# A two-block transformer kernel: the second mixer and the expert choice in two halves of the tokens, and two token tiles instead of one by gathered expert rows

## The chip, the cores and the metric

The kernel runs on one core of a Trainium2 chip. Its time is the device time of one execution in microseconds (us). A core has five engines with a queue of instructions each: TensorE (PE in the profile; PEld is its weight load), VectorE (DVE), ScalarE (ACT), GpSimd (POOL) and SyncE (SP), which here only issues transfers. Sixteen DMA engines move data between device memory (HBM) and on-chip memory. TensorE writes its products to eight accumulator banks (PSUM), each 128 partitions by 512 fp32 numbers.

## The reference

512 tokens of 1024 numbers pass two blocks, all in fp32. Block one is feed-forward, an attention mixer, feed-forward. Block two is a mixer (latent attention with 8 heads beside a retention with a state carried over chunks of 128 tokens) and then PEER, a layer of 16384 experts, each a row `u` and a row `v` of 1024 numbers:

```python
q = (xt @ w_query).reshape(T, 8, 2, 128)
s = einsum('thpd,pkd->thpk', q, sub_keys)          # 2 x 128 keys
s_top, i_top = top_k(s, 16)                        # level 1
cand = s_top[:, :, 0, :, None] + s_top[:, :, 1, None, :]
best, pos = top_k(cand.reshape(T, 8, 256), 16)     # level 2: the expert choice
eidx = ...                                         # i_top0 * 128 + i_top1, at pos
g = softmax(best)
a = gelu(einsum('thkd,td->thk', expert_u[eidx], xt))
out = einsum('thk,thkd->td', g * a, expert_v[eidx])
```

So each token uses 8 x 16 = 128 of the 16384 experts. The output is the normalised sum of the block's input and this.

## The kernel before, in words

The 512 tokens are four tiles of 128 (tiles 0 to 3). Every fp32 weight product is three products of high and low parts (`mm3`, L126 to L128): a weight tile is brought in by SyncE (`raw`, L113), and split by ScalarE into a high part (`whi`, L120) and by VectorE into the rest (`wlo`, L121).

Block one ends at about 1270 us. The second mixer (`mixer2`) runs over all four tiles: projections, attention by pairs of tile and head, retention, and the output product (`project`), with each tile normalised and transposed behind it (`boundary`). Queries and level 1 (`peer_queries`, `peer_level1`) make, for each tile, head and key half, scores on TensorE and the 16 best with VectorE (L1344 to L1348). Level 2 (`peer_level2`) is VectorE work, tile by tile.

The experts are done in two ways:

- Tiles 1 to 3 are dense: all 16384 experts for all 384 tokens, in 128 chunks of 128 experts. `emit_a(c)` splits one chunk of `u` rows (`in_euT`) and makes its products with 384 columns: 8 x 3 matmuls. The main loop over chunks multiplies the result by a gate table (`gt`, read from `dg` in device memory, L1543), splits the product and the chunk of `v` rows (`in_evp`) and adds to six accumulator halves (`acc`): 3 tiles x 2 halves x 3 matmuls of 512 columns. `peer_spread` builds the gate table of a tile out of one-hot rows on VectorE (L1375 to L1378) and 128-wide fp16 products.
- Tile 0 is gathered: GpSimd fetches, for each of the 128 places of the choice, one row for each token (`erow`, L1446, 128 rows of 4 KB, 512 KB in all). A `u` row is multiplied with the normalised tokens and summed by one VectorE instruction (L1450, here called a dot), a `v` row is added with its weight by another (L1458).

The first 78 chunks of `emit_a` run while VectorE does level 2 and the spread; all but 12 of them go to device memory (`da`) and come back in the main loop, where `emit_a` is 12 chunks ahead of `acc`. The pace of gathers is written out: `gathers(rate, after)` issues rows when enough are owed. A scheduler then sets the order in each queue, from the order of the code, its priorities and the free buffers.

Of the kernel before, what the change touches and what calls it, by code (L numbers as in the profile page):

```python
# [20 lines left out]
P = 128  # L21
S = 512
# [6 lines left out]
NF = 22  # L29
NEG = -1.0e30  # L30
# [51 lines left out]
class Body:  # L82
# [33 lines left out]
    def split(self, r, room=None):  # L116
# [4 lines left out]
        self.last_low = self.nc.vector.tensor_tensor(lo, r, hi.bitcast(F32), op=OP.subtract)  # L121
        return hi, lo
# [35 lines left out]
    def xrstd(self, t):  # L158

        return self.rstd(self.sumsq(self.xe[:, t, :D + 1], D), eps=0.0)  # L160

    def diag(self, r):

        d = self.misc.tile([P, P], F32, name="dg", tag="dg")
        self.nc.scalar.activation(d, self.idf, AF.Copy, scale=r)
        return d

    def ndiag(self, c, n):
        return self.diag(self.rstd(self.sumsq(c, n)))


    def setup(self):
# [12 lines left out]
        c = self.const  # L185
        self.front = ExitStack()
# [3 lines left out]
        self.xe = f.tile([P, NT, D + 4], F32, name="x")  # L190
        self.x = self.xe[:, :, :D]
        self.nc.vector.memset(self.xe[:, :, D:], (EPS * D) ** 0.5)
# [152 lines left out]
    def begin(self, hi, lo):  # L345
# [4 lines left out]
        with ExitStack() as st:  # L350
# [11 lines left out]
            def turned(q):  # L362
                qs = slice(2 * q, 2 * q + 2)
                self.acol(0, 1, "g_pre_ffn1", qs)
                for t in range(NT):
                    self.transposed(self.x[:, t, q * 256:(q + 1) * 256], 2, t, hi, lo, self.ac[:, 0, qs],
                                    self.mc[:, 0, qs], 2 * q, diag=dg[t])
# [11 lines left out]
            for t in range(NT):  # L379
                nc.sync.dma_start(self.x[:, t, :], a["x"][t * P:(t + 1) * P, :])  # L380
# [22 lines left out]
    def h_tiles(self):  # L403
        hi = self.hbuf.tile([P, KD, S], F32R, name="h_hi", tag="h_hi")
        lo = self.hbuf.tile([P, KD, S], F32R, name="h_lo", tag="h_lo")
        return hi, lo

# [32 lines left out]
    def boundary(self, join, scale, bias, last):  # L440


        d, h = {}, []

        def turn(t):
            if t == 0:
                h.extend(self.h_tiles())
            self.transposed(self.x[:, t, :], KD, t, *h, self.ac[:, scale], self.mc[:, bias], diag=d.pop(t))

        for t in range(NT):  # L450
            last(t)
            join(t)
            d[t] = self.diag(self.xrstd(t))
            if t in (1, 2):
                turn(t - 1)
        return h, [lambda: turn(2), lambda: turn(3)]

    def postnorm(self, t, y, grow):
# [6 lines left out]
        for hf in range(2):  # L465
# [3 lines left out]
            nc.vector.tensor_tensor(self.x[:, t, sl], self.x[:, t, sl], v, op=OP.add)  # L469


    def ffn(self, gu, dn, h, between, join, scale, bias, ps0=None):
# [3 lines left out]
        with ExitStack() as st:  # L476
# [12 lines left out]
            for f in range(NF):  # L489
# [5 lines left out]
                for n, cut in enumerate(cuts):  # L495
                    for j in range(2):
# [3 lines left out]
                        if not f and not n:  # L500
                            late_h[j]()
# [26 lines left out]
            for f in range(NF):  # L528
# [7 lines left out]
                if f < NF - 6:  # L536
                    for t in range(NT):
# [3 lines left out]
                                 lambda t: product(t, ws, by_half if t < NT - 1 else by_chunk))  # L541
# [1162 lines left out]
```

## Time and profile before

| | us |
|---|---|
| median of 3 runs (2862.94, 2867.7, 2869.01) | 2867.7 |
| the profiled execution | 2865.86 |
| its span in the profile | 2864.1 |
| TensorE busy | 2805.2 |
| VectorE busy | 2052.6 |
| ScalarE busy | 1158.3 |
| GpSimd busy | 366.7 |

The span is the stretch from the first to the last recorded instruction. "Busy" is the sum of an engine's recorded instructions; overlapping matmuls count once. DMA share is the mean busy share of the sixteen DMA engines, GB/s what they moved.

The program after 1270 us has three stages that are used below: the second mixer with its output product and the normalisations at its edges (to 1605 us), queries, both levels of choice and the spread beside the first 78 `emit_a` (to 2104 us, where the first `acc` product starts), and the main loop with the end (to 2864.1 us).

### The profile page before, as it was taken

The numbers are of one execution on the slowest core, as the hardware profiler recorded it, in microseconds if no ns is written. First come the engines' busy times: TensorE is split into PE (matmuls) and PEld (weight loads), VectorE is DVE, ScalarE is ACT, GpSimd is POOL, SyncE is SP. The second block draws the span as 40 slices with busy tenths as digits, with TensorE's granted clock in tenths as the row PEclk, the third lists the DMA queues.
The fourth block names the chain that finished last, engine by engine and source line by source line (L and its number), as shares of the span: only waits on it lengthen the run. The fifth ranks groups of instructions, "written<-read, shape, count | busy, mean of one in ns | idle before, by whom it ended". The sixth has DMA issues, their size and how long they took to land. (4 is left out here: it accounts for less than half of the span.)

```text
span 2864.1 us, 41177 instructions
## 1 busy us (share of the span) xinstructions
PE 2805.2 (98%) x15725; PEld 2414.2 (84%) x15725; DVE 2052.6 (72%) x4416; ACT 1158.3 (40%) x1946; POOL 366.7 (13%) x367
## 2 busy tenths in 40 slices
PE   8999999999999999999999999999999999999998
PEld 6877788869788877888898989899988888898996
DVE  6795246785655787225665699999967778787887
ACT  4343145333534444225522433655633333333333
POOL 0000000000000000001001001111121115433441
PEclk9999999999999999999997999999999999999999
DMA  7663221212033564321121226888899999888885
GB/s 277 226 226 138 103 74 60 92 60 89 16 138 121 194 235 177 110 103 41 67 79 47 104 78 225 295 282 314 318 334 342 324 311 358 317 314 317 298 328 193
DMA packets 152533, 553.09 MB, mean 193 GB/s; under 512 B 12368, under 2 KB 61840, under 8 KB 112400
## 3 DMA queue, kind: packets, MB, share of 16 engines
q1 hardware_dynamic: 111040, 404.25, 38.8%
q0 software_dynamic: 38848, 140.56, 13.8%
q10 hardware_dynamic: 2448, 5.65, 0.5%
q8 instruction: 123, 2.02, 0.3%
q14 instruction: 74, 0.61, 0.1%
HBM read 505.95 MB, written 44.47 MB: 192 GB/s over the span
## 5 line engine op out<-in xcount | busy, mean ns | idle before, releaser
L120 ACT ACTIVATE whi<-raw 128x1024 fp32r<-128x1024 f32 (+2 forms) x491 | 510.1, 1040 | 806.0 <-PE ps L127 385.8
L121 DVE TENSOR_TENSOR wlo<-raw,whi 128x1024 fp32r<-128x1024 f32 (+2 forms) x491 | 588.7, 1199 | 299.2 <-ACT whi L120 295.6
L126 PE MATMUL ps<-h_hi,whi 128*128 128x384 f32 (+2 forms) x1904 | 691.1, 364 | 4.7 <-ACT ga L1431 3.1
L127 PE MATMUL ps<-h_lo,whi 128*128 128x384 f32 (+2 forms) x1904 | 684.2, 359 | 0.8 <-DVE h_lo L132 0.8
L128 PE MATMUL ps<-h_hi,wlo 128*128 128x384 f32 (+2 forms) x1904 | 683.0, 359 | 0.7 <-DVE wlo L121 0.7
L126 PEld LDWEIGHTS ps<-h_hi,whi 128*128 128x128 f32 x1904 | 359.2, 189 | 37.7 <-ACT ga L1431 3.8
L128 PEld LDWEIGHTS ps<-h_hi,wlo 128*128 128x128 f32 x1904 | 359.1, 189 | 32.4 <-DVE wlo L121 1.3
L127 PEld LDWEIGHTS ps<-h_lo,whi 128*128 128x128 f32 x1904 | 359.8, 189 | 31.3 <-DVE h_lo L132 1.0
L126 PE MATMUL acc<-whi,wh 128*128 128x512 f32 x768 | 304.0, 396 | 1.7 <-ACT wh L131 1.7
L128 PE MATMUL acc<-whi,wl 128*128 128x512 f32 x768 | 304.0, 396 | 0.3 <-DVE wl L132 0.3
L127 PE MATMUL acc<-wlo,wh 128*128 128x512 f32 x768 | 303.8, 396 | 0.1
L1446 POOL DMA_INDIRECT erow<-in_eu,ids x128 | 141.8, 1108 | 648.8 <-DVE junk L1450 478.3
L131 ACT ACTIVATE wh<-wv 128x384 fp32r<-128x384 f32 x128 | 67.2, 525 | 341.1 <-issue 174.4
L1446 POOL DMA_INDIRECT erow<-in_ev,ids x128 | 166.2, 1299 | 225.2 <-DVE eacc L1458 198.5
L126 PE MATMUL ps<-whi,h_hi 128*128 128x256 f32 (+1 forms) x608 | 186.0, 306 | 0.0
L127 PE MATMUL ps<-wlo,h_hi 128*128 128x256 f32 (+1 forms) x608 | 184.0, 303 | 0.0
L128 PE MATMUL ps<-whi,h_lo 128*128 128x256 f32 (+1 forms) x608 | 183.7, 302 | 0.0
L128 PEld LDWEIGHTS acc<-whi,wl 128*128 128x128 f32 x768 | 144.5, 188 | 35.9 <-DVE wl L132 0.8
L126 PEld LDWEIGHTS acc<-whi,wh 128*128 128x128 f32 x768 | 144.3, 188 | 35.1 <-ACT wh L131 2.0
L127 PEld LDWEIGHTS acc<-wlo,wh 128*128 128x128 f32 x768 | 144.5, 188 | 33.3 <-DVE wlo L121 0.5
L1458 DVE SCALAR_TENSOR_TENSOR eacc<-erow,wgt,eacc 128x1024 f32<-128x1024 f32 x127 | 162.8, 1282 | 6.3 <-DMA erow<-in_ev,ids 3.2
L290 DVE SCALAR_TENSOR_TENSOR rows<-mraw,sil,rows 128x256 f32<-128x256 f32 x336 | 159.8, 481 | 6.5
(453 smaller groups left out, 4636.3 us busy)
## 6 DMA issues: line engine op xcount, KB each, us to landing
raw<-in_euT SPq DMA_DIRECT2D x64, 1024.0 KB
raw<-in_evp SPq DMA_DIRECT2D x64, 1024.0 KB
raw<-in_gu SPq DMA_DIRECT2D x44, 1024.0 KB
mraw<-in_wmod SPq DMA_DIRECT2D x24, 1024.0 KB
mraw<-in_wada SPq DMA_DIRECT2D x24, 1024.0 KB
dg<-gb SPq DMA_DIRECT2D x24, 1024.0 KB
gt<-dg SPq DMA_DIRECT2D x16, 1536.0 KB
raw<-in_dn SPq DMA_DIRECT2D x22, 1024.0 KB
```

What stands on the lines that cost most here:

```text
L120: self.nc.scalar.activation(hi, r, AF.Copy)
L121: self.last_low = self.nc.vector.tensor_tensor(lo, r, hi.bitcast(F32), op=OP.subtract)
L126: mm(out, l[0], r[0], start=start, stop=False)
L127: mm(out, l[0], r[1], start=False, stop=False)
L128: self.last_mm = mm(out, l[1], r[0], start=False, stop=stop)
L131: self.nc.scalar.activation(hi, v, AF.Copy)
L290: nc.vector.scalar_tensor_tensor(rows, rv[:, k, :], c, rows, op0=OP.mult, op1=OP.add)
L1446: nc.gpsimd.indirect_dma_start(out=row, out_offset=None, in_=src, in_offset=bass.IndirectOffsetOnAxis(ap=ids[:, m:m + 1], axis=0))
L1458: nc.vector.scalar_tensor_tensor(eacc, row, wg[:, m:m + 1], eacc, op0=OP.mult, op1=OP.add)
```

## The change

Block one stays. The rest is done for two halves of the tokens, `self.tt` = tiles (0, 1), then (2, 3). For tiles 0 and 1: mixer, output product (`project_half`), queries, level 1 and level 2 (`chosen`). Then the same for tiles 2 and 3, with `hook` asking for gathers of `u` rows after each split (2.0 rows) and each attention step (0.8 x 2.0). The mixer's and the query weights are brought in and split once for each half, and the keys, values and states of the first half are kept for the second. Tiles 0 and 1 are both gathered: 256 `u` rows with a dot each, and 256 `v` rows. The `v` rows are summed on TensorE, four rows in a step: eight products 32 columns wide and 512 long, one for each row and half, into four column groups of the array and two accumulator banks (`ga`), with weights spread on diagonals (`zw`). They begin when all `u` rows are done. The dense part is left with tiles 2 and 3: 256 columns in `emit_a`, four `acc` halves, 16 instead of 24 parts of the gate table. At the edges of the mixers a tile is scaled first (half on ScalarE, half on VectorE) and then transposed, where before one product with a diagonal matrix did both.

```diff
-                self.mm3(p[:, :384], (w[0][:, ks], w[1][:, ks]), (h[0][:, k, P:], h[1][:, k, P:]), k == 0, k == KD - 1)
+                self.mm3(p[:, :W], (w[0][:, ks], w[1][:, ks]), (h[0][:, k, :], h[1][:, k, :]), k == 0, k == KD - 1)
...
+        RU, RD, RW = 1.2, 2.0, 0.7
...
+        rows = gp.tile([P, 4, D], F32, name="rows")
+        self.slots += [rows[:, j] for j in range(4)]
...
+    def gather_u(self, n):
+        t, m = divmod(n, P)
+        row = self.slots[n % len(self.slots)]
+        nc.gpsimd.indirect_dma_start(out=row, out_offset=None, in_=self.a["eu"],
+                                     in_offset=bass.IndirectOffsetOnAxis(ap=self.ids[t][:, m:m + 1], axis=0))
+        junk = self.misc.tile([P, D], BF, name="junk", tag="sg")
+        nc.vector.scalar_tensor_tensor(junk, row, 1.0, self.x(t), op0=OP.mult, op1=OP.mult,
+                                       accum_out=self.act[t][:, m:m + 1])
...
+        def fetch(k):
+            t, j = divmod(k, 32)
+            held[k] = [self.slots[(4 * k + g) % 8] for g in range(4)]
+            for g in range(4):
+                nc.gpsimd.indirect_dma_start(out=held[k][g], out_offset=None, in_=a["ev"],
+                                             in_offset=bass.IndirectOffsetOnAxis(ap=self.idt[t][:, 32 * g + j:32 * g + j + 1], axis=0))
+        def weigh(k):
...
+            for hf in range(2):
+                for g in range(4):
+                    nc.tensor.matmul(y[t][hf][32 * g:32 * g + 32, :], z[:, j % 8, g, :], held[k][g][:, hf * 512:hf * 512 + 512],
+                                     start=j == 0, stop=j == 31)
...
+        def values(rate, after):
+            if self.got < 2 * P:
+                return
+            owed += rate
+            while done < min(owed, 64):
+                with tc.issue_after(after.ins):
+                    fetch(done)
+                if done:
+                    with tc.issue_after(self.last_mm.ins):
+                        weigh(done - 1)
+                done += 1
...
             if c < P - 3 or c == P - 1:
-                for t in range(3):
+                for t in range(2):
...
-            gathers(R2 if c < EARLY - LEAD else R3 if c < P - LEAD else R4 if c < P - TAIL else 2 * P, pace)
+            if self.got < 2 * P:
+                self.gathers(RD, pace)
+            else:
+                values(RW if c < P - FIN - 2 else 99, pace)
...
+                self.tt = (0, 1)
+                h = self.second(0, hs[0], late, old)
+                sp, v, ix = self.select(0, *h, s1)
+                self.tt = (2, 3)
+                z = self.hbuf.tile([P, 4, D], F32, name="slots", tag="h_hi")
+                self.slots = [z[:, j] for j in range(4)]
...
+                with self.later(600):
+                    for t in range(2):
+                        self.chosen(sp, t, self.peer_level2(sp, v[t], ix[t]), "ps")
+                self.hook = lambda n, after: self.gathers(n * R0, after)
+                h = self.second(1, hs[1], [], old)
```

The order of VectorE at the expert choice of the first tile, before (`cand`, `best`, `bp` are the choice, `wlo` the split of a weight tile, here of `emit_a`):

```order
L1348 MAX_INDEX pix_14951<-pv_14948,t_15966 128x8
L121 TENSOR_TENSOR wlo<-raw,whi 128x1024
L1290 TENSOR_TENSOR cand<-pv_14760 128x8x16
L1291 TENSOR_TENSOR cand<-pv_14760 128x8x56
...
L1347 MAX_INDEX bp<-best,cand 128x8
L1348 MAX_INDEX bp<-best,t_16213 128x8
L121 TENSOR_TENSOR wlo<-raw,whi 128x1024
L1344 MAX best<-cand 128x8 x2
```

And the end of the choice of the second tile in the changed program (`ids` and `idt` are the lists of rows, `pa` is the second half's projection):

```order
L1406 TENSOR_TENSOR oh<-oh 128x256
L1407 TENSOR_TENSOR gi_14324<-oh 128x128
L1479 SCALAR_TENSOR_TENSOR idsf<-gi_14302,gi_14324 128x128
L1480 CAST ids_11460<-idsf 128x128
L1484 CAST idt_11462<-ps 128x128
L122 TENSOR_TENSOR wlo<-raw,whi 128x1024
L605 TENSOR_TENSOR rt<-pa_14370,cos 128x16
```

Before, a split stands after every few rows of the choice; now the choice of tiles 0 and 1 stands in one piece, with four dots and no split in it, between three splits of the second half's first weights and the next.

The order of VectorE in the attention of the second half (`mx` and `neg` are the row maximum and its negative, `pT` the transposed probabilities):

```order
L629 TENSOR_REDUCE mx<-ps 128x1 x2
L630 TENSOR_SCALAR neg<-mx 128x1
L1494 SCALAR_TENSOR_TENSOR junk,act_11465<-slots,x_87 128x1024
L630 TENSOR_SCALAR neg<-mx 128x1
L142 COPY pT<-sc 128x384
L1494 SCALAR_TENSOR_TENSOR junk,act_11465<-slots,x_87 128x1024 x2
L629 TENSOR_REDUCE mx<-ps 128x1 x2
```

A dot stood nowhere in the mixer before; now one or two follow each step of a head. In the whole program 541 splits stand where 491 did, and 176 dots stand ahead of the first use of the gate table in the main loop, where 49 did.

The order of TensorE in the main loop of the changed program, at a step of values, with buffer numbers (the first three rows end the products of one chunk, the last begin the next):

```order
L129 MATMUL acc_21243<-whi_22390,wh_22386 128x512
L130 MATMUL acc_21243<-wlo_22391,wh_22386 128x512
L131 MATMUL acc_21243<-whi_22390,wl_22387 128x512
L1640 MATMUL ga_22372<-rows_21222,zw_22374 32x512 x4
L1640 MATMUL ga_22373<-rows_21222,zw_22374 32x512 x4
L129 MATMUL acc_21240<-whi_22428,wh_22422 128x512
L130 MATMUL acc_21240<-wlo_22429,wh_22422 128x512
```

And GpSimd's where the `u` rows end and the `v` rows begin:

```order
L1491 DMA slots_14072<-in_eu,ids1_11460 128x1024 x4
L1491 DMA rows_21222<-in_eu,ids1_11460 128x1024 x4
L1626 DMA slots_14072<-in_ev,idt0_11461 128x1024 x4
L1626 DMA rows_21222<-in_ev,idt0_11461 128x1024 x4
```

The first products of `v` rows stand behind those of chunk 36, and 64 such steps stand in the rest of the loop; the sums of 128 `v` rows on VectorE (L1458) are gone.

## Rows read from the trace of the kernel before

**Rows 1.** The page, busy time of each engine.
```profile
PE 2805.2 (98%) x15725; PEld 2414.2 (84%) x15725; DVE 2052.6 (72%) x4416; ACT 1158.3 (40%) x1946; POOL 366.7 (13%) x367
```

**Rows 2.** Stretches: length, PE, PEld, DVE, ACT, POOL busy (count), PEclk, DMA share, GB/s.
```profile
1270.00:1605.00 335.00, 325.61 (x2287) 297.68 (x2286) 196.27 (x519) 134.60 (x299) 27.97 (x50) 0.94 0.19 68
1605.00:2104.00 499.00, 486.92 (x3261) 459.11 (x3259) 450.00 (x1400) 262.62 (x339) 63.75 (x58) 1.00 0.69 242
1735.00:2085.00 350.00, 342.18 (x2449) 329.97 (x2449) 332.57 (x840) 207.07 (x257) 59.92 (x52) 1.00 0.83 293
2104.00:2864.10 760.10, 749.12 (x3504) 642.09 (x3504) 606.78 (x747) 266.25 (x373) 252.55 (x212) 0.99 0.86 313
```

**Rows 3.** Timeline of TensorE: start, us, engine, line, operation, tiles, shape, count.
```profile
1470.08 0.28 PE L128 MATMUL ps<-whi,h_lo 128*128 128x256 f32 x1
1470.20 0.28 PE L126 MATMUL ps<-whi,h_hi 128*128 128x256 f32 x1
...
2441.76 0.33 PE L127 MATMUL ps<-h_lo,whi 128*128 128x384 f32 x1
2441.93 0.34 PE L128 MATMUL ps<-h_hi,wlo 128*128 128x384 f32 x1
2442.11 0.39 PE L126 MATMUL acc<-whi,wh 128*128 128x512 f32 x1
2442.34 0.39 PE L127 MATMUL acc<-wlo,wh 128*128 128x512 f32 x1
```

**Rows 4.** VectorE groups by form: count | busy us, mean ns | idle before.
```profile
L121 DVE TENSOR_TENSOR wlo<-raw,whi 128x1024 fp32r<-128x1024 f32 x456 | 556.1, 1220 | 270.1 <-ACT whi L120 266.6 <-PE sc L1383 1.3
L1450 DVE SCALAR_TENSOR_TENSOR junk<-erow,xr 128x1024 bf16<-128x1024 f32 x128 | 155.2, 1217 | 6.4 <-DMA erow<-in_eu,ids 6.4
...
L1543 DVE TENSOR_TENSOR wv<-ga,gt 128x384 f32<-128x384 f32 x128 | 71.2, 557 | 12.9 <-DMA gt<-dg 9.1
...
L1376 DVE TENSOR_TENSOR oj<-io,jt 128x1024 f16<-128x1024 f16 x48 | 32.7, 682 | 0.1
```

**Rows 5.** VectorE groups of 1270 to 1605, then of 1605 to 2104 us.
```profile
L121 DVE TENSOR_TENSOR wlo<-raw,whi 128x1024 fp32r<-128x1024 f32 x29 | 35.4, 1222 | 33.4 <-ACT whi L120 33.3
...
L1450 DVE SCALAR_TENSOR_TENSOR junk<-erow,xr 128x1024 bf16<-128x1024 f32 x50 | 60.8, 1216 | 2.6 <-DMA erow<-in_eu,ids 2.6
```

**Rows 6.** Expert choice of one tile: the stretch, and the splits in it.
```profile
1734.20:1763.00 28.80, 27.83 (x161) 27.51 (x160) 28.56 (x133) 12.62 (x17) 0.00 (x0) 1.00 0.51 158
...
L121 DVE TENSOR_TENSOR wlo<-raw,whi 128x1024 fp32r<-128x1024 f32 x7 | 8.5, 1211 | 0.0
```

**Rows 7.** Three stretches with much transfer: columns as in rows 2.
```profile
20.00:40.00 20.00, 18.60 (x164) 12.54 (x165) 12.58 (x32) 8.78 (x21) 0.00 (x0) 1.00 1.02 422
2120.00:2160.00 40.00, 40.00 (x173) 32.21 (x172) 31.06 (x47) 13.70 (x19) 7.80 (x8) 1.00 1.05 390
2400.00:2600.00 200.00, 200.00 (x1004) 180.00 (x1003) 162.43 (x176) 70.34 (x97) 85.14 (x65) 1.00 0.87 322
```

**Rows 8.** The page, DMA issues: count and KB of one.
```profile
raw<-in_evp SPq DMA_DIRECT2D x64, 1024.0 KB
gt<-dg SPq DMA_DIRECT2D x16, 1536.0 KB
```

**Rows 9.** TensorE at 38 us: eight products 32 columns wide, then the next.
```profile
38.01 1.07 PE L281 MATMUL mod<-raw,cp 128*32 128x256 f32 x16
39.01 0.50 PE L126 MATMUL ps<-h_hi,whi 128*128 128x512 f32 x1
```

**Rows 10.** First row gather of the timeline; dots by tile, min/median/max, first, last.
```profile
1763.03 1.08 POOL L1446 DMA_INDIRECT erow<-in_eu,ids  x1 [143.07 <-issue]
...
L1450 DVE SCALAR_TENSOR_TENSOR junk<-erow,xr x128: 1205/1218/1227, 1768.6 to 2421.6; 128x1024 bf16<-128x1024 f32 x128
```

**Rows 11.** A stretch of mixer two with a lower granted clock (PEclk).
```profile
1540.00:1580.00 40.00, 40.00 (x254) 37.30 (x255) 22.25 (x54) 9.87 (x16) 3.80 (x6) 0.76 0.23 80
```

**Rows 12.** Chain that ended last, its first piece after TensorE.
```profile
2852.83 0.02 issue
```

More of the change, by code (lines that the diff above doesn't have):

```diff
@@ L185, in setup @@
         c = self.const
+        self.tt = tuple(range(NT))
+        self.hook = None
+        self.xa = self.pool(ctx, "xa", side="right")
         self.front = ExitStack()
@@ L438, in transposed, with boundary, norm, third @@
             self.to_pair(v[:, :m, :], hi[:, sl, ts], lo[:, sl, ts])
-    def boundary(self, join, scale, bias, last):
-        d, h = {}, []
+    def boundary(self, join, scale, bias, last, halves=()):
+        nc = self.nc
+        d, h = {}, {}
         def turn(t):
[L446 to L450, printed above, removed]
+            b = t // 2 if halves else 0
+            if b not in h:
+                h[b] = self.half(b) if halves else self.h_tiles()
+            self.transposed(d.pop(t), KD, t % 2 if halves else t, *h[b], self.ac[:, scale], self.mc[:, bias])
+        def norm(t, r):
+            d[t] = self.misc.tile([P, D], F32, name="xs", tag="xn", bufs=1)
+            nc.scalar.activation(d[t][:, :512], self.x(t)[:, :512], AF.Copy, scale=r)
+            nc.vector.tensor_scalar(d[t][:, 512:], self.x(t)[:, 512:], r, None, op0=OP.mult)
+        n = len(self.tt)
+        for i, t in enumerate(self.tt):
             last(t)
             join(t)
[L453 to L456, printed above, removed]
+            r = self.xrstd(t)
+            if 1 <= i <= max(1, n - 2):
+                turn(self.tt[i - 1])
+            if i <= max(1, n - 2):
+                norm(t, r)
+        if n == 2:
+            return h[halves[0]], [(1, lambda: turn(t))]
+        def third():
+            turn(2)
+            norm(3, r)
+        return h if halves else h[0], [(0, third), (1, lambda: turn(3))]
     def postnorm(self, t, y, grow):
@@ L548, in nform @@
         kh = 1024 // width
-        out = [self.ps() for _ in range(NT)]
+        nt = len(self.tt)
+        late = dict(late or ())
+        wait = bool(late)
+        out = [self.ps() for _ in range(nt)]
         ws = []
@@ L563, in nform @@
             ws = []
-        for t in range(NT):
+        for t in range(nt):
             then(t, out[t][:, :width])
@@ L587, in attend @@
         l, r, masks, vals = seg
-        w = r.shape[-1]
+        w = sum(z.shape[-1] for z in r)
         got = {}
@@ L1171, in ret_mix @@
         dec = self.rc["dec"][:, 2 * hh:2 * hh + 2]
-        for n in range(3):
+        for l, n in enumerate(self.tt):
+            if n == NT - 1:
+                continue
             p = self.ps("po")
@@ new lines, in gathers, with select @@
+    def gathers(self, rate, after):
+        self.owed += rate
+        with self.tc.issue_after(after.ins):
+            while self.got < min(2 * P, self.owed):
+                self.gather_u(self.got)
+                self.got += 1
+    def select(self, b, h, late, st):
+        nc = self.nc
+        sp = self.pool(st, "sel", reuse_waits="tile")
+        v = [sp.tile([P, 16, 16], F32, name=f"pv{t}") for t in range(2)]
+        ix = [sp.tile([P, 16, 16], U32, name=f"pix{t}") for t in range(2)]
+        with ExitStack() as s1:
+            self.peer_level1(self.pool(s1, "sel1", reuse_waits="tile"), h, v, ix, late, lambda: None)
+        return sp, v, ix
@@ L1460, in peer @@
-        self.owed = 0.0
-        self.got = 0
-        def gathers(n, after):
-            self.owed += n
-            with tc.issue_after(after.ins):
-                while self.got < 2 * P and self.got < self.owed:
-                    gather(self.got)
-                    self.got += 1
         nxt = 0
```

489 lines of the change are left out of this document (276 added, 213 removed).

## The prediction

> **What bounds the kernel now.** I read the busy times first, then the same by stretch, then single instructions. TensorE is busy 98% of the span [rows 1] and 97% to 99% in each of the three stages after 1270 us [rows 2], so up to now it is the bound. But VectorE is not far behind where the expert choice and the gate table are built: 450 of 499 us, and 332.6 of 350 in the inner part, 95% [rows 2]. In the main loop the transfers are next: 313 GB/s at a DMA share of 0.86 over the whole stage [rows 2]. So whatever is taken from TensorE there is worth only what these two leave. What a difference of this kernel can tell from no change is 0.2%, about 6 us.
>
> **What TensorE is rid of.** A product of 384 columns takes 0.17 to 0.18 us from start to start, one of 256 takes 0.12, one of 512 0.23 [rows 3]. `emit_a` has 128 x 24 = 3072 products: 3072 x 0.055 = 169 us less. A third of the `acc` products goes, 768 x 0.233 = 179 us, and a third of the spread, some 18 us by 256 of its 768 narrow products at 0.07, which is my estimate from half of the 0.12. Added are 64 steps of values with 8 products each, 32 columns wide. Eight such products with 256 columns took 1.0 us until the next one began [rows 9]; with 512 columns I take 2.0, in all 128 us. TensorE's balance is 169 + 179 + 18 - 128 = 238 us less. Were nothing else to bind, the time would be 2866 - 238 = 2628.
>
> **Up to the end of the first half's mixer.** Block one is the same up to 1270 us. The scaled copies at the edges cost VectorE and ScalarE half a tile each, at most 12 x 1.2 us by the row of the split [rows 4], and stand where VectorE has 139 of 335 us idle [rows 2]: from 0 to 15 us, taken at 0. Half of the mixer's 335 us [rows 2] is 168, so the first half ends at 1438 us. VectorE does all of the mixer's splits in it (35.4 us, [rows 5]) and half of its other work, (196.3 - 35.4) / 2 = 80: 116 us, covered by TensorE's 168.
>
> **From there to the first `acc` product.** Here VectorE takes the lead. Its work from 1270 us to this point was 196 + 450 = 646 us [rows 2]. To it come 50 repeated splits (541 against 491 in the order) at 1.22 = 61, and 126 more dots (176 against 50, [rows 5]) at 1.22 = 154 [rows 4]. One of three gate tables goes: four groups like the row of 32.7 us, a third of 131 = 44. That is 646 + 61 + 154 - 44 = 817, less the 116 above: 701 us. TensorE has in the same stretch the other 168 us of the mixer and 487 less 78 x 24 x 0.055 = 103 less 18: 534 us. So this stage is VectorE's. At the 95% that it reached where it was nearly the bound [rows 2] it takes 701 / 0.95 = 738 us and the first `acc` product starts at 2176 us; before it was 2104. The ends are 100% (2139) and the 90% of the whole stage before (2217). The order also shows why VectorE can't be packed better at one place: the choice of tiles 0 and 1 is one piece with no split in it. One tile's choice takes 28.6 - 8.5 = 20 us of VectorE [rows 6], two and four dots 45 us, in which TensorE has only three splits' worth of products. This is idle time of TensorE, inside the 701 us and not to be added.
>
> **The main loop while `u` rows are left.** 80 of 256 rows are left, and by the order the first `v` step stands behind chunk 36. A row gather moves 0.524 MB, a chunk's share of a weight load as much (1024 KB for two, [rows 8]), a gate table part 16/24 of 1.57 MB = 1.05 [rows 8], and a pair of `da` chunks 0.26. So 37 chunks move 41.9 + 19.4 + 5.2 + 4.8 = 71 MB. What is the rate? In 2400 to 2600 us 322 GB/s went at a share of 0.87, which is 370 at a full share; in 2120 to 2160 us 390 were carried at 1.05, and 422 in 20 to 40 us, with other, longer pieces [rows 7]. I take 380, between the two of the main loop: 188 us. VectorE has 80 x 1.22 + 37 x (1.22 + 2 x 0.37) = 170 us here, the 0.37 being two thirds of 0.557 [rows 4]; TensorE 37 x 12 x 0.233 = 103. The transfers end last. Ends: 170 (VectorE) and 71 / 0.322 = 221.
>
> **The main loop with `v` rows.** Chunks 37 to 127 need 91 x 12 x 0.233 = 254 us of TensorE, the last 50 `emit_a` 50 x 24 x 0.12 = 144, the steps 128: 526 us. VectorE needs only some 240: 141 splits at 1.22 and 91 x 0.74. The 128 sums have left it. But the transfers are 134 MB of `v` rows, 47.7 + 26.2 of weights, 11.5 of gate table and 3.8 from `da`: 223 MB. In 526 us that would be 425 GB/s, more than any stretch of the trace carried. At 380 it takes 588 us. Ends: 529 at 422 GB/s and 694 at the 322 that the loop did carry. The change takes 348 us of products from TensorE and adds 128 rows of `u` and 128 of `v`, 134 MB, while the weights of the dense part must be read as before, since 256 tokens want all experts as 384 did. That is where I see the gain go.
>
> [...]
>
> **The sum.** From the last `acc` product to the end of the span it was 2864.1 - 2852.8 = 11 us [rows 12], and the last tiles end in the same way. 1438 + 738 + 188 + 588 + 11 = 2963. The profiled execution was 1.8 us longer than its span (2865.9), and the median 1.8 longer again: 2966, I say 2965.
>
> **Rivals.**
>
> 1. The queues keep up, and TensorE or VectorE is the bound everywhere: 422 GB/s in the main loop [rows 7] and VectorE at 100% in the middle. 2139 + 170 + 529 + 11 + 4 = 2853, faster by 15 us. For it speaks the 422; against it that this stretch has another kind of transfer, and that VectorE was never seen above 95% over a long stretch. It is faster than before only if both hold, the main loop above some 415 GB/s: then VectorE's 701 us must also be smaller than I count for anything near 2628. Chance 0.14 for all below 2860.
> 2. Each step waits for its rows. `v` rows have two sets of four buffers, and a set is free only after its products on TensorE. Four issues at 1.08 us, a landing of 1768.6 - 1763.0 - 1.1 = 4.5 us after the last issue [rows 10], and 2.0 us of products make 10.8 us for a step that hides nothing, 64 x 10.8 = 691 instead of 588: 3068. Two sets ought to hide half; but with all DMA engines full a landing is longer than that of the first row at 1763 us. TensorE waits at the step's first product, and all of the next chunk's `acc` stands behind it in its queue; GpSimd's next fetch waits for it in turn. It decides where a landing takes over 12 us. Chance 0.16.
> 3. The four column groups don't run side by side. Then a step takes four times 2.0 us, TensorE has 398 + 512 = 910 us in the last stage, and the time is 3287. Rows 9 speak against it: 8 narrow products in 1.0 us. Chance 0.03.
> 4. TensorE's clock. [...] Chance 0.07.
>
> **How the numbers follow.** The forecast, VectorE in the middle and transfers in the main loop, has 0.60, with its own range from 2890 to 3030; the rivals have 0.14, 0.16, 0.03 and 0.07. The range 2850 to 3080 leaves out the bottom of the first rival, the third, and the worst of the second and fourth. Below 2862 lie the first rival's cases: faster 0.14. Within 0.2%, 2862 to 2873, lies the thin edge between it and the forecast: 0.05. Slower: 0.81.
>
> **What would show it.** Right: the first `acc` product near 2176 us with VectorE over 93% busy between 1438 us and there and TensorE near 75%; in the last 600 us a DMA share near 1 at 370 to 390 GB/s, TensorE waiting at `acc` for splits whose weights landed late, or at `ga` for rows. Wrong: the first `acc` product before 2120 us (the VectorE count), over 410 GB/s in the loop (the rate), a share well under 0.9 with long waits at `ga` (rival 2), steps of 8 us (rival 3), or TensorE still above 95% to the end.

## The result

| | before | changed |
|---|---|---|
| median, us | 2866.65 (4 runs) | 3155.05 (4 runs, 3149.3 to 3160.96) |
| ratio | 1 | 1.1007, interval 1.0991 to 1.1024 |
| span of the profiled execution, us | 2864.1 | 3153.4 |

It is slower by 288 us, on the side that was forecast, and three times as much as forecast (2965, range to 3080). In the page of the changed kernel (the busy times, then the forty slices of clock and DMA share):

```profile
PE 2766.9 (88%) x15970; PEld 2213.3 (70%) x15970; DVE 2056.7 (65%) x4593; ACT 1149.3 (36%) x1963; POOL 679.1 (22%) x626
...
PEclk9999999999999999998777789989899899999998
DMA  6562212120435632243348665879999998899994
```

TensorE is now at 88% where it had 98% [rows 1]. Its busy time hardly fell, 2805 to 2767 us, for two reasons that are seen below. The last stage has 621 us of it where 526 were forecast, and part of the work ran at a lower granted clock: PEclk has four sevens and four eights in slices 19 to 29, where before there was a single seven. The stages of the changed kernel, in the columns of [rows 2], in the order: first half's mixer; choice of tiles 0 and 1; second half's mixer; early chunks; loop with `u` rows; loop with `v` rows; and all from 1270 us to the first `acc` product at 2310:

```profile
1270.00:1470.00 200.00, 172.64 (x1164) 156.99 (x1162) 132.43 (x325) 99.52 (x210) 20.85 (x36) 0.91 0.32 113
1540.00:1600.00 60.00, 9.03 (x51) 8.59 (x51) 50.41 (x271) 3.19 (x7) 8.44 (x10) 0.53 0.22 72
1600.00:1865.00 265.00, 191.72 (x1095) 173.37 (x1095) 212.51 (x446) 75.39 (x144) 128.95 (x110) 0.76 0.73 252
1935.00:2310.00 375.00, 287.27 (x2315) 272.19 (x2314) 317.11 (x645) 169.79 (x231) 127.56 (x98) 0.90 0.86 315
2310.00:2503.00 193.00, 121.70 (x452) 87.93 (x454) 148.47 (x248) 51.57 (x76) 91.92 (x70) 0.89 0.92 339
2503.00:3130.00 627.00, 620.81 (x3316) 384.62 (x3315) 259.57 (x337) 191.99 (x286) 273.35 (x250) 1.00 0.93 345
1270.00:2310.00 1040.00, 783.23 (x5589) 730.43 (x5588) 830.76 (x2224) 404.99 (x661) 288.12 (x256) 0.85 0.62 222
```

Two things are to be seen. Up to 2310 us no engine is full: VectorE has 831 of 1040 us, and behind the first half's mixer 698 of 840, 83%, where 95% was forecast from the inner stretch in [rows 2]; TensorE has 783 at a clock of 0.85. Behind 2503 us TensorE is busy 99% and the DMA engines 0.93 at 345 GB/s, both.

The sum of the forecast against this trace (the first query product of the first half came at 1469.6 us, the first `acc` product at 2310.1, the first `v` step at 2502.9, the last `acc` product at 3129.5):

| stage | forecast | measured | difference |
|---|---|---|---|
| 1270 to the end of the first half's mixer | 168 | 200 | +32 |
| to the first `acc` product | 738 | 840 | +102 |
| 37 chunks with `u` rows | 188 | 193 | +5 |
| the rest with `v` rows | 588 | 627 | +39 |
| end | 11 | 24 | +13 |

VectorE's waits up to 2310 us, and TensorE's (engine, what waits, for what: us in all, times, longest):

```profile
DVE wlo L122 <- ACT whi L121: 66.9, 37, 11.4
DVE junk L1494 <- DMA slots<-in_eu,ids: 44.2, 35, 4.7
```

```profile
PE ps L129 <- ACT ga L1550: 55.0, 31, 12.2
PE ps L1483 <- DVE idsf L1479: 54.6, 2, 27.8
```

At L1483 a list of rows is turned by TensorE. Two such products stand in its queue ahead of the second half's, and wait 55 us together for the choice on VectorE; before, no wait of TensorE in this part was over 4 us in all.

TensorE's timeline in the loop with `v` rows shows a whole step (the first line) and then one whose products are broken up:

```profile
2558.72 1.93 PE L1640 MATMUL ga<-rows,zw 128*32 128x512 f32 x16
2560.58 0.50 PE L129 MATMUL acc<-whi,wh 128*128 128x512 f32 x1
2560.92 0.40 PE L130 MATMUL acc<-wlo,wh 128*128 128x512 f32 x1
2561.16 0.39 PE L131 MATMUL acc<-whi,wl 128*128 128x512 f32 x1
...
2563.25 0.40 PE L131 MATMUL acc<-whi,wl 128*128 128x512 f32 x1
2563.58 1.91 PE L1640 MATMUL ga<-slots,zw 128*32 128x512 f32 x8
2565.42 0.50 PE L129 MATMUL acc<-whi,wh 128*128 128x512 f32 x1
2565.85 1.90 PE L1640 MATMUL ga<-slots,zw 128*32 128x512 f32 x4
2567.69 0.50 PE L130 MATMUL acc<-wlo,wh 128*128 128x512 f32 x1
...
2569.51 1.90 PE L1640 MATMUL ga<-slots,zw 128*32 128x512 f32 x4
2571.34 0.50 PE L131 MATMUL acc<-whi,wl 128*128 128x512 f32 x1
```

Between `acc` products it is 0.23 us from start to start, as in [rows 3]. A narrow product leaves two records (1024 at L1640 for the 512 products of 64 steps). The 16 records from 2558.72 are the eight products of a whole step, 1.86 us until the next product starts. The four records from 2565.85 are two products, and take 1.84 us; the eight records before them, four products, take the same. The step that was laid out as 8 products in one piece stands in three, and the order has 102 pieces for 64 steps. Each change between narrow and wide costs some 0.1 us besides, 0.33 and 0.34 where 0.23 is usual.

The chain that ended last begins later too (start, us, what):

```profile
3129.84 0.17 DVE ssum L1609
...
3135.65 0.60 POOL fin L1596
3136.26 7.27 issue
...
3144.91 0.66 DVEq L1867
```

In [rows 12] the last chunk was followed by the end of three tiles whose old values were there. Now tile 1's end comes with those of tiles 2 and 3, and there are two buffers for old values. The last load of them (L1596) is issued only at 3135.65, after tile 1's output was sent off at 3132.51, and the addition that needs it starts on VectorE at 3140.26. The 7.27 us of the chain hold this wait and the small steps behind it; before, the same place had 3.82 us.

### The profile page after: what moved, and what is told of

It reads as the page before. It is cut to its first block, busy times and chain, and to the rows that moved or that the text cites. A ratio compares the mean times of both kernels' runs of the same rounds, so it can differ in the third digit from the quotient of the medians.

```text
span 3153.4 us, 42454 instructions
## 1 busy us (share of the span) xinstructions
PE 2766.9 (88%) x15970; PEld 2213.3 (70%) x15970; DVE 2056.7 (65%) x4593; ACT 1149.3 (36%) x1963; POOL 679.1 (22%) x626
## 5 line engine op out<-in xcount | busy, mean ns | idle before, releaser
L121 ACT ACTIVATE whi<-raw 128x1024 fp32r<-128x1024 f32 (+2 forms) x541 | 561.0, 1040 | 1046.4 <-PE ps L130 345.0
L129 PE MATMUL ps<-half,whi 128*128 128x256 f32 x1280 | 382.3, 299 | 65.4 <-ACT ga L1550 55.0
L1491 POOL DMA_INDIRECT slots<-in_eu,ids x220 | 283.9, 1290 | 551.5 <-DVE junk L1494 411.3
L131 PE MATMUL ps<-half,wlo 128*128 128x256 f32 x1280 | 376.8, 295 | 21.1 <-DVE wlo L122 21.0
L130 PE MATMUL ps<-half,whi 128*128 128x256 f32 x1280 | 374.3, 293 | 3.3 <-DVE half L135 3.1
L129 PE MATMUL ps<-h_hi,whi 128*128 128x512 f32 (+1 forms) x848 | 335.2, 396 | 1.3 <-DVE v L445 1.1
L129 PEld LDWEIGHTS ps<-half,whi 128*128 128x128 f32 x1280 | 256.9, 201 | 106.6 <-ACT ga L1550 61.7
L130 PE MATMUL ps<-h_lo,whi 128*128 128x512 f32 (+1 forms) x848 | 329.9, 389 | 0.1
L131 PE MATMUL ps<-h_hi,wlo 128*128 128x512 f32 (+1 forms) x848 | 328.0, 387 | 0.0
L1494 DVE SCALAR_TENSOR_TENSOR junk<-slots,x 128x1024 bf16<-128x1024 f32 x220 | 265.5, 1219 | 48.2 <-DMA slots<-in_eu,ids 47.7
L131 PEld LDWEIGHTS ps<-half,wlo 128*128 128x128 f32 x1280 | 256.5, 201 | 25.2 <-DVE wlo L122 24.7
L130 PEld LDWEIGHTS ps<-half,whi 128*128 128x128 f32 x1280 | 256.5, 200 | 5.4 <-DVE half L135 3.8
L130 PEld LDWEIGHTS ps<-h_lo,whi 128*128 128x128 f32 x848 | 160.1, 189 | 28.1 <-DVE h_lo L135 0.5
```

Source lines behind the costliest of these rows:

```text
L121: self.nc.scalar.activation(hi, r, AF.Copy)
L129: mm(out, l[0], r[0], start=start, stop=False)
L130: mm(out, l[0], r[1], start=False, stop=False)
L131: self.last_mm = mm(out, l[1], r[0], start=False, stop=stop)
L1491: nc.gpsimd.indirect_dma_start(out=row, out_offset=None, in_=self.a["eu"], in_offset=bass.IndirectOffsetOnAxis(ap=self.ids[t][:, m:m + 1], ...
L1494: nc.vector.scalar_tensor_tensor(junk, row, 1.0, self.x(t), op0=OP.mult, op1=OP.mult, accum_out=self.act[t][:, m:m + 1])
```

## The experiments

Each of the 15 runs below is the changed kernel with the edit that is shown or named. All were executed once, with a profile, but for e_all, which was executed four times. Kernels before on the same chips: 2862.2, 2866.6, 2868.2 and 2863.9 us. "acc" is the first `acc` product, "v" the first step of values, "last" the last `acc` product, all in us of the profile. The first four kernels of the table are alike up to "acc", which came between 2306 and 2310: a difference of 4 us there says nothing.

| kernel | time | acc | v | last |
|---|---|---|---|---|
| changed | 3155.1 | 2310 | 2503 | 3129 |
| e_onepiece | 3121.6 | 2310 | 2502 | 3095 |
| e_noweigh | 3108.2 | 2306 | 2498 | 3086 |
| e_nofetch | 3042.8 | 2307 | 2502 | 3030 |
| e_dotsonly | 3036.0 | 2233 | 2385 | 3013 |
| e_gatheronly | 3047.8 | 2201 | 2370 | 3022 |
| e_nou | 2860.2 | 2106 | 2210 | 2838 |
| e_floor | 2624.3 | 2103 | 2207 | 2612 |
| e_flooridt | 2600.1 | 2079 | 2183 | 2589 |
| e_idtlate | 3141.0 | 2293 | 2488 | 3115 |
| e_nohook | 3212.6 | 2344 | 2550 | 3181 |
| e_storeq | 3161.5 | 2314 | 2506 | 3136 |
| e_slots5 | 3132.3 | 2284 | 2479 | 3107 |
| e_slots3 | 3186.9 | 2346 | 2532 | 3161 |
| e_halfrow | 3092.7 | 2270 | 2439 | 3067 |
| e_all | 3109.2 (4 runs) | 2299 | 2492 | 3083 |

**The last stage: the pieces, the products, the transfers.**

```diff
-                for g in range(4):
+                for g in (3, 2, 1, 0):
                     nc.tensor.matmul(y[t][hf][32 * g:32 * g + 32, :], z[:, j % 8, g, :], held[k][g][:, hf * 512:hf * 512 + 512],
```

> The changed kernel with one edit: in each step of values the product of the row that is fetched last is issued first, so that the eight products stand side by side in the order (64 pieces instead of 102). In the changed kernel the stage from the first step to the last product took 626 us (2502 to 3129), with TensorE busy nearly all of it, and a piece took 1.85 us whether it held 2 or 8 products. Theory P (TensorE is the bound there, and pays each piece anew): 38 pieces x 1.85 us = 70 us and as many changes of shape less, the stage at about 550 us, the time at about 3080. Theory D (the transfers are the bound there): 223 MB at some 375 GB/s is 595 us, so no more than 30 us less, the time at 3125 or above.

e_noweigh makes the products only where `j in (0, 31)`, and so leaves out most of the values:

> The changed kernel without 60 of the 64 steps' products (first and last step of each tile stay); all rows are still fetched. It leaves out most of the values of tiles 0 and 1. Theory P: TensorE has only acc and u products, some 400 us, in the stage of 626, and the time falls by 150 us or more unless the transfers hold it. Theory D: 223 MB at 375 GB/s, 595 us, the time at about 3125; with the fetches no longer waiting for TensorE, the transfers may run nearer to 390 GB/s, 570 us and 3100.

e_nofetch fetches only where `k < 2`, and makes all products on the rows that are there:

> The changed kernel with 2 of the 64 fetches of v rows; all the products are made, on the rows that are there, and stand in 60 pieces of the order instead of 102. The stage from the first step to the last acc product was 626 us, 591 with the products in 64 pieces, and 588 without 60 steps' products. If the transfers were its bound in the last two, it falls to TensorE's own sum, 398 + 60 x 2.0 = 518 us, the time to about 3045; if TensorE or the order of the loop was the bound, it stays above 570.

From "v" to "last" the stage took 627 us in the changed kernel and 593, 588 and 528 in these. The three stages in the columns of [rows 2], first e_onepiece, as a whole, then its first 200 us and 200 us near its end:

```profile
2502.00:3092.00 590.00, 549.09 (x3300) 374.49 (x3296) 256.30 (x329) 190.41 (x282) 275.39 (x250) 0.97 0.98 366
2500.00:2700.00 200.00, 166.22 (x858) 97.54 (x856) 79.24 (x112) 51.18 (x76) 95.06 (x92) 0.92 1.00 372
2860.00:3060.00 200.00, 200.00 (x1295) 148.10 (x1295) 94.04 (x115) 74.63 (x110) 95.25 (x82) 1.00 0.99 377
```

e_noweigh:

```profile
2498.00:3086.00 588.00, 444.01 (x2354) 366.28 (x2352) 253.62 (x339) 190.37 (x288) 273.18 (x249) 0.87 0.94 368
```

e_nofetch:

```profile
2502.00:3030.00 528.00, 528.00 (x3315) 370.75 (x3308) 263.96 (x344) 192.36 (x291) 3.06 (x5) 1.00 0.48 165
```

With the products whole, TensorE is busy 549 of 590 us and the DMA engines 0.98 at 366 GB/s; with hardly any products TensorE has 444, and the time is nearly the same: the transfers end last, as theory D has it (3121.6 us missed its 3125 by 3, theory P's 3080 by 42). Without the transfers the stage is TensorE's alone, 528 of 528 (expected 518). So the transfers hold the stage at some 590, and the broken steps put TensorE above it, at 621 to 627. Theory P had the direction in the changed kernel, and too much of a gain from mending it. The margin is thin: in its first 200 us e_onepiece has full DMA engines and TensorE busy 166 us, near its end both are full.

**The rows of `u`: both, dots alone, fetches alone, none.** e_nou returns from `gather_u` unless `m % 64 == 0` or `m == P - 1`, with 0 for the scores left out; e_dotsonly issues the gather once for each buffer, and its dots read what lies there; e_gatheronly makes nearly all dots 8 numbers long:

```diff
-        nc.vector.scalar_tensor_tensor(junk, row, 1.0, self.x(t), op0=OP.mult, op1=OP.mult,
+        q = slice(0, 8 if m < P - 1 else D)
+        nc.vector.scalar_tensor_tensor(junk[:, q], row[:, q], 1.0, self.x(t)[:, q], op0=OP.mult, op1=OP.mult,
```

> The changed kernel with 6 of the 256 u rows and their dots only; it leaves out most of the scores of tiles 0 and 1. The first acc product came at 2310 us. Theory V (VectorE and the transfers hold the second half's stage because of the rows): 176 dots at 1.3 us and 92 MB leave the stage before it, and the first acc product comes near 2100; with the 80 rows of the main loop gone too (192 us for 37 chunks become about 105 us of TensorE) the time is near 2860. Rival W (running the mixer and the choice in halves costs TensorE waits of its own, whatever the rows do): the first acc product stays above 2230 and the time above 2990.

> The changed kernel with all 256 dots, on rows that were fetched once for each buffer: 248 row gathers of u are left out, and the scores are not those of the choice. It takes the transfer of the u rows away and leaves their VectorE work. If VectorE's time is what held the middle, the first acc product stays within 40 us of 2310; if the transfers (329 GB/s at a share of 0.89 from 2000 to 2300 us) or the dots' waits for rows held it, it comes at 2230 or before. The 37 chunks with rows left then take VectorE's 170 us instead of 192.

> The changed kernel with all 256 u rows fetched, but each dot only over the first 8 of 1024 numbers (the last of a tile is whole); the scores are not those of the choice. The first acc product came at 2310 us with rows and dots, at 2233 with dots on rows fetched once, at 2106 with neither. Theory V (the dots' VectorE time is most of it, and the rows' transfer is felt because VectorE waits): rows without dots leave it below 2160. Rival T (the transfer by itself holds the stage, weights of u arriving late because the queues are full): above 2200. After it, the loop's stage of 37 chunks, 192 us, falls to about 140 by V, since VectorE loses 96 us there, and stays above 180 by T.

Without rows the first `acc` product comes 204 us earlier, at 2106, and the kernel takes 2860: theory V's numbers nearly to the point. Dots alone add 127 us to it, fetches alone 95, both 204. The fetches alone, at 2201, are just on T's side of its 2200, and 41 from V's 2160; dots alone, at 2233, missed "within 40 us" by 37 and the other mark, 2230, by 3. So neither is most of it: they nearly add up. The 37 chunks of the loop took 152 us with dots alone (170 expected) and 169 with fetches alone, between V's 140 and T's 180. What VectorE does meanwhile is read in its busy time of the stage. Without rows and values (e_floor, below), dots alone, fetches alone:

```profile
1270.00:2103.00 833.00, 709.12 (x5590) 672.59 (x5589) 627.11 (x1865) 403.89 (x662) 52.31 (x74) 0.92 0.46 165
```

```profile
1270.00:2233.00 963.00, 753.70 (x5596) 701.97 (x5595) 829.10 (x2228) 406.48 (x661) 50.05 (x69) 0.88 0.39 140
```

```profile
1270.00:2201.00 931.00, 736.91 (x5584) 694.51 (x5583) 636.66 (x2222) 402.23 (x661) 264.60 (x256) 0.88 0.67 248
```

VectorE is without work 833 - 627 = 206 us in the first, 134 in the second, 294 in the third, and 1040 - 831 = 209 in the changed kernel; before it was 834 - 646 = 188 [rows 2]. Dots alone fill 72 us of its idle time; with the fetches they fill none. The same from 1470 us, where the queries of the first half begin, to the first `acc` product; first the changed kernel, then dots alone, then e_floor:

```profile
1470.00:2310.00 840.00, 610.59 (x4426) 573.44 (x4426) 698.33 (x1899) 305.47 (x452) 267.27 (x220) 0.84 0.70 248
1470.00:2233.00 763.00, 582.68 (x4427) 546.67 (x4428) 694.65 (x1902) 307.04 (x451) 29.18 (x33) 0.87 0.41 147
1470.00:2103.00 633.00, 538.75 (x4427) 516.90 (x4428) 493.55 (x1537) 305.02 (x452) 30.49 (x38) 0.92 0.51 181
```

With dots alone VectorE is busy 695 of 763 us, 91%; the fetches bring 77 us more, in which it has nearly nothing more to do.

**The price of halves.** e_floor is e_nou with e_noweigh's and e_nofetch's edits; it leaves out nearly all of the experts of tiles 0 and 1.

> The changed kernel with 6 of 256 u rows, 2 of 64 fetches of v rows and 4 of 64 steps of products; it leaves out nearly all of the experts of tiles 0 and 1. What stays is the price of halves and of a dense part for 256 tokens. TensorE has 128 us less to do than in the run with no u rows (2860 us), where the last stage had 625 us for 526 of TensorE. If the transfers of v rows and the pieces of their products held that stage, it falls to some 400 us and the time to 2640; if the weights of the dense part hold it (halves leave their own waits there too), it stays above 480 and the time above 2710.

It took 2624 us, and its last stage 405 us with TensorE busy all of it (forecast without products: 398): the dense part for 256 tokens is as cheap as it was worked out. But the first `acc` product stays at 2103, where TensorE's own work of the forecast, 1438 + 534, would have given 1972. Of these 131 us, some 30 are the first half's mixer, and most of 53 the choice; the rest is spread over queries and early chunks, and was not taken apart. In e_floor, the choice and the second half's mixer:

```profile
1537.00:1590.00 53.00, 6.59 (x40) 6.35 (x41) 45.81 (x264) 1.68 (x3) 4.83 (x5) 0.53 0.15 50
1590.00:1755.00 165.00, 148.98 (x1102) 138.04 (x1101) 110.84 (x270) 75.63 (x145) 14.27 (x22) 0.94 0.33 115
```

TensorE works 7 of 53 us, at a granted clock of 0.53. The two turned lists at the head of its queue were moved behind the second half's queries in e_idtlate (the changed kernel) and e_flooridt (e_floor):

```diff
-        p = self.ps(tag)
-        nc.tensor.transpose(p[:, :P], idf, self.idf)
-        nc.vector.tensor_copy(self.idt[t], p[:, :P])
...
                 self.hook = None
+                for t in range(2):
+                    self.turned_ids(t)
```

> The changed kernel with one edit: the two turned lists of rows (needed by the fetches of v rows alone) are made behind the second half's queries instead of behind the choice. In the changed kernel TensorE waited 55 us for the choice at these two small transposes, with all of the second half's products behind them in its queue; in the new order 10 splits stand within the choice, where none stood. If this head of the queue cost the time that TensorE waited, the first acc product comes 40 to 55 us before 2310 and the time falls by as much. Rival: VectorE's sum up to there is the same, 2310 moves by less than 20 us, and what is gained at the choice is lost behind it.

> The run without rows and values (2624 us, first acc product at 2103) with the two turned lists made late, so that no small product waits for the choice at the head of TensorE's queue. With the u rows in, this edit won 17 us of the 55 that TensorE waited there. If those 55 us were hidden there by VectorE's own sum, they come out here, where VectorE is free: first acc product at 2065 or before. If VectorE's 46 us of choice in one stretch bind whatever stands in the queue, it stays above 2085.

The first `acc` product came 17 us earlier in the one and 24 in the other, of 55 and 50 that TensorE had waited there. The rival of the first run named the amount (under 20). In the second the result, 2079, lies between the two. The rest of the wait is not gone but stands at the next product that needs VectorE, a small one on `pa` behind the choice; e_idtlate, then e_flooridt:

```profile
PE sc L428 <- DVE pa L167: 43.8, 3, 37.7
PE sc L428 <- DVE pa L167: 28.5, 2, 28.3
```

So about half was the queue's head in e_flooridt, and the rest VectorE's choice in one stretch.

**Where the rows stand, and what makes them late.** e_nohook sets R0 to 0 and RU to 2.4; e_storeq issues the stores of `da` and `dg` with `nc.scalar.dma_start`.

> The changed kernel with no u rows in the second half's mixer and twice as many for each early chunk (R0 0 instead of 2.0, RU 2.4 instead of 1.2); 183 dots instead of 176 stand ahead of the first use of the gate table. The mixer of the second half (1600 to 1865 us with rows, 1590 to 1755 in the run without any) must then take about 165 us. If rows cost their VectorE and transfer time wherever they stand (sum), what is won there, 100 us, is lost in the early chunks, and the first acc product stays within 30 us of 2310. If they cost more in the mixer, where each dot stands in the chain of a head's small steps, it comes before 2270; if more beside the weights' loads, after 2350.

> The changed kernel with the stores of early results (da) and of the gate table (dg) issued from ScalarE's queue instead of SyncE's. From 1935 to 2310 us SyncE waited 135 us for ScalarE's gelu at these stores with the loads of u weights behind them, and ScalarE waited 93 us for those loads. If that order of one queue is what makes the weights late, the first acc product comes 30 us or more before 2310. If full DMA engines (share 0.86, near 1 in the last third) make them late, it moves by less than 12 us either way.

In e_nohook the second half's mixer takes 170 us, where 165 were expected (columns as in [rows 2]):

```profile
1600.00:1770.00 170.00, 152.61 (x1112) 141.81 (x1111) 108.76 (x259) 75.39 (x139) 10.17 (x16) 0.92 0.35 122
```

It wins 107 us up to the queries' choice (last of level 1 at 1826 instead of 1934), and loses 141 in the early chunks: 2344, 34 later, with 7 dots more (9 us) in it. That is 4 us outside the mark of the sum, and short of the 2350 of the other: the rows cost about their sum wherever they stand, a little more beside the weights' loads. e_storeq changes nothing (4 us later): the stores in SyncE's queue are not what makes the weights late. ScalarE waits 99 us for them there, 93 in the changed kernel, and SyncE now waits 289 us for a weight buffer to be split (L114 for `wlo`). More weight buffers were not tried. That leaves the rows' way in. e_slots5 and e_slots3 give the rows five and three buffers up to the main loop; e_halfrow fetches half of each row after a buffer's first use, from the table seen as 32768 rows of 512 numbers.

```diff
-                self.slots = [z[:, j] for j in range(4)]
+                self.base = [z[:, j] for j in range(4)]
+                self.slots = self.base + [z2]          # e_slots5; e_slots3: self.base[:3]
```

> The changed kernel with five buffers for u rows instead of four up to the main loop (nine instead of eight buffers are not used in the loop, which keeps its eight). In the changed kernel VectorE waits 44 us for rows at dots up to 2310 us, and 67 us at splits for weights. Theory B (rows are late because a fetch starts only when a dot four rows earlier has ended): one more row ahead takes 15 us or more from 2310. Theory Q (rows and weights are late because the DMA engines are full): less than 8 us either way.

> The same with three buffers up to the main loop. Theory B: the first acc product at 2340 or later. Theory Q: within 15 us of 2310.

> The changed kernel with only the first half of each u row fetched after the first use of each buffer (2 KB instead of 4 for each of 128 tokens), the dots still over 1024 numbers; the scores are not those of the choice. The number of fetches and of dots is the same. Rows cost 77 us up to the first acc product beyond the dots (2310 against 2233 with rows fetched once). Theory Q: by bytes, half of it comes back, 2272, and the 37 chunks fall from 193 us to near 170. Theory B or a price for each fetch: 2295 or later.

The dots of VectorE up to the first `acc` product, their last columns the idle time ahead of them and what ended it: changed kernel (and its splits), then five buffers, then three:

```profile
L1494 DVE SCALAR_TENSOR_TENSOR junk<-slots,x 128x1024 bf16<-128x1024 f32 x187 | 226.5, 1219 | 44.7 <-DMA slots<-in_eu,ids 44.2
L122 DVE TENSOR_TENSOR wlo<-raw,whi 128x1024 fp32r<-128x1024 f32 x171 | 207.4, 1218 | 67.2 <-ACT whi L121 66.9
```

```profile
L1494 DVE SCALAR_TENSOR_TENSOR junk<-slots,x 128x1024 bf16<-128x1024 f32 x187 | 225.6, 1218 | 11.0 <-DMA slots<-in_eu,ids 10.5
```

```profile
L1494 DVE SCALAR_TENSOR_TENSOR junk<-slots,x 128x1024 bf16<-128x1024 f32 x186 | 226.3, 1220 | 103.4 <-DMA slots<-in_eu,ids 103.2
```

Idle time ahead of dots goes from 45 to 11 us with one buffer more and to 103 with one less, and the first `acc` product from 2310 to 2284 and 2346: theory B. Half the bytes bring it to 2270, 40 of 77 us, and the loop's 37 chunks to 169 us: what theory Q said of bytes. The landings in the traces join the two. The last column is the median in us from issue to landing in the early chunks, first in e_nofetch, which is the changed kernel up to there (DMA share 0.86 from 1935 to 2307), then in e_halfrow (0.74 from 1935 to 2270):

```profile
raw<-in_euT SPq DMA_DIRECT2D x35, 1024.0 KB, 7.9
slots<-in_eu,ids POOLq DMA_INDIRECT x91, 7.7
raw<-in_euT SPq DMA_DIRECT2D x33, 1024.0 KB, 6.3
slots<-in_eu,idd POOLq DMA_INDIRECT x85, 6.0
```

A load of weights, the same in both, takes 7.9 us beside whole rows and 6.3 beside half rows; in e_floor, without rows, 5.6. So the same load took longer with more carried beside it (5.6, 6.3 and 7.9 us), and four buffers did not cover a row's 7.7 us: VectorE waited 44 us for rows. Where five buffers took 34 us of the dots' waits away, the splits' waits stayed (76 us).

**Together.** e_all has e_onepiece, e_idtlate and e_storeq.

> The changed kernel with three edits together: products of values in 64 pieces, turned lists late, stores of da and dg from ScalarE's queue. Alone the first gave 33 us and the second 14. If they add up and the third gives nothing: 3155 - 47 = 3108. If the transfers eat the gains of the middle, since the last stage then asks for more at once: 3120. With 30 us of the third: 3080. None makes it as fast as the kernel before, 2867.

It took 3109.2 us (4 runs, 3098 to 3116; ratio to before 1.084, interval 1.0803 to 1.0877): as the sum has it. No run with all rows and values in it comes near the kernel before, and e_floor shows why: 2867 - 2624 leaves 243 us for rows and values, which cost 3155 - 2624 = 531.

## Why the prediction was wrong

- **The step that failed: the stage up to the first `acc` product, 738 us as 701 of VectorE over 0.95, with no term for transfers.** VectorE's work was right: 817 us were worked out from 1270 us on, 831 measured (187 dots in it, not 176). But the stage behind the first half's mixer took 840 us, with VectorE busy 698 of them, 83%. e_dotsonly parts the 102 us. With the same dots and no row fetches the stage took 763 us with VectorE at 91%: 25 us are waits of VectorE that the 0.95 of an inner stretch [rows 2] did not have, in a stage with attention, level 1 and the choice in one piece. The other 77 us come with the row fetches. I counted transfers only from the first `acc` product on and put them at nothing ahead of it, but from 1935 to 2310 us they were at a share of 0.86 and 315 GB/s. Half the bytes give 40 of the 77 back, a fifth buffer 26.
- **Idle time carried over comes nearer, but by luck.** VectorE was idle 188 us up to this point before, and 209 in the changed kernel with 831 us of work. 1270 + 817 + 188 = 2275 is nearer to 2310 than 2176 is. But by the same rule dots alone give 1270 + 829 + 188 = 2287, and they came at 2233: VectorE's idle time shrank to 134 us there, and the fetches, which the rule does not know, brought the rest back.
- **TensorE's idle time at the choice, "not to be added": wrong by some 17 us,** which e_idtlate won. Without rows the halves' waits show in full: in e_floor TensorE is busy 539 and VectorE 494 of 633 us, neither is full, and the stage is 99 us over TensorE's forecast of 534.
- **The dense part, which TensorE is partly rid of: right.** In e_floor the two stages of the loop took 104 and 405 us, 103 and 398 worked out. A whole step of values takes 1.86 us (2.0 forecast).
- **The half of the mixer: too small by 32 us.** 335 us was halved, but the last products of block one run until 1300 us and stand in the first half once, which makes some 15. And TensorE waited 27 of the 200 us, where it had 9 of 335: 9 of them for the scaled tiles of the new edges (`xs`, L464), whose price I had taken at 0. The second half, without rows, took 165 us, so the two halves take 30 us more than the whole.
- **The loop with `u` rows: the time right, 188 against 193 us, its terms not.** 71 MB at 380 GB/s were counted; 339 GB/s for 193 us are 65 MB, since 69 rows were left and not 80. The two errors cancel. VectorE had 148 us there, not 170.
- **The loop with `v` rows: 588 us forecast, 593 with whole steps.** The bound is right; here too the bytes (223 MB, where 366 GB/s for 590 us are 216) and the rate (380) were both 3 to 4% too high. The changed kernel took 34 us more, for broken steps: rival 3's place, with another mechanism. The four column groups do run side by side in a whole step, eight products in 1.86 us; but a piece of two products, in one group by the code, takes as long, 1.84 us. The order of the changed program has 102 pieces; I had quoted a whole one.
- **The end: 13 us more,** part of it a load of old values behind two buffers.
- **Rivals.** 1 failed on both its conditions: VectorE was busy 83% of the stage up to the first `acc` product, and e_onepiece carried 366 GB/s at a share of 0.98. The most that 200 us of this loop carried in these runs was 407 at 1.03 (e_noweigh, 2860 to 3060 us), more than my 380, but less than the 415 that the rival needs. 2 did not come: TensorE waited 6 us for rows in the last stage, though 40 in e_onepiece, where the steps are whole. 4, a lower granted clock, came in another place than in [rows 11]: it fell to 0.76 in the second half's mixer, where TensorE had 192 of 265 us.

What stays open: what VectorE's and TensorE's waits in the halves are made of, beyond the choice; and how much of the middle's loss is the lower clock. In the middle TensorE was busy 783 us at a granted clock of 0.85, in e_floor, with the same products, 709 at 0.92. But waits do not always come with a lower clock: in the loop with `u` rows of e_dotsonly TensorE had 111 of 152 us, at 1.00.

## What to carry to other kernels

Count the transfers in every stage, and not only where they look like the bound: here row fetches ahead of the main loop cost 77 us beside VectorE's full work, through rows and weights that landed later. A busy share read from one inner stretch is not that of a stage with chains through several engines (0.95 was read, 0.91 came without fetches, 0.83 with them), and the idle time of the stage before is no better a term: dots filled 72 of its 206 us when nothing was fetched, and none when rows were. Moving one more tile from dense to gathered took 238 us from the bound engine by the forecast's count, and put 134 MB on queues that were at a share of 0.86 in that loop. And in a written order look at all the places of a pattern, not at the first.

## What the runs showed of the hardware

A piece of narrow fp32 products (128 x 32 weights, 512 columns) takes 1.86 us for eight in four column groups, and 1.84 us for two, which by the code are in a single group. The DMA engines at a share of 0.98 carried 366 GB/s of row gathers and weight loads together (e_onepiece), against 390 at 1.05 and 422 at 1.02 in [rows 7]. A weight load of 1 MB took 5.6 us from issue to landing at a share of 0.74 and 263 GB/s (e_floor, 1826 to 2103 us), 7.9 at 0.86 and 319 (e_nofetch, 1935 to 2307 us) and 9.9 at 0.97 and 376 (e_gatheronly, 1935 to 2201 us), medians all. In the 60 us of the choice TensorE, busy 9 us, had a mean granted clock of 0.53 of full speed.
